# A transposed q and k: split into high and low parts in front of the transpose, or on the way out of PSUM

## The chip, the cores and the metric

The kernel runs on one core of one Trainium2 chip. The metric is the device time of one execution in microseconds (us). Engines: TensorE (PE, with its weight loads as PEld), VectorE (DVE), ScalarE (ACT), GpSimd (POOL) and SyncE (SP, which issues most DMAs).

## The reference

One decoder layer on x of 1024 tokens by 1024 features, in fp32: an RMS norm, one input projection, two attention mixers side by side, a SiLU gate on each, an output projection and the residual. What matters here:

```
proj = rms_norm(x, norm_gain) @ w_in                       # 4420 columns, split
qa, ka = rms_norm(qa, q_norm_a), rms_norm(ka, k_norm_a)    # per head of 64, 8 heads
qb, kb = rms_norm(qb, q_norm_b), rms_norm(kb, k_norm_b)    # the same for mixer B
# A: an indexer scores all causal keys; each query keeps its 256 best keys
logits = q . k * 64 ** -0.5 + bias;  p = softmax(logits)   # over the kept keys
# B: the same with three dilated windows in place of the kept keys
out = x + concat(a * silu(za), b * silu(zb)) @ w_out
```

## The kernel before

**Precision.** TensorE works on fp32r operands. An fp32 number is kept as a high part (the number rounded to fp32r) and a low part (number minus high part). A projection is three matmuls: high x high, high x low, low x high (L416 to L418). For the scores the 64 features of a head fill half of the 128 rows, so high and low part lie one above the other: k's stationary form is [high; low], q comes as [high; low] and as [low; high], and two matmuls of 128 rows give all four products (L537, L538).

**Work.** The 16 heads make 8 pairs; the order is the four pairs of mixer B, then the four of mixer A. For each pair 8 blocks of 128 tokens are projected, two blocks (a "duo") at a time. When a duo's projection is done, `finish` brings it to SBUF (`raw`), takes sums of squares, splits v and multiplies k by the norm weights of k and q together (`gk`, one row of 64 in all partitions, L448). `finish2` multiplies k by its inverse norm (L456), splits it into high and low part (L458 on ScalarE, L459 on GpSimd) and makes q (L462). `later` transposes the four 128x128 pieces of k and copies them out of PSUM (L471, L475). The queries of a duo are split by `split_q` (L502, L503) into high, low, high of 64 columns each, and `transpose_q` transposes columns 0 to 127 and 64 to 191 of each head and block (L512, L513), in two PSUM tiles, each copied out by ScalarE (L515).

Attention runs in 64 units: a pair, a duo of queries, one head. `scores` takes score chunks of up to 512 keys, adds the bias (VectorE, L544; for mixer A GpSimd first adds the selection mask, L542) and takes the exp (L554). `pt` transposes the probabilities as fp32 (L571), ScalarE copies out the high part (L575), VectorE the low part (L576); `pv` multiplies with v (L587, L589). `combine` (L609) adds up, gates and stores.

**The selectors.** For mixer A the 256 best keys of each query are found by a search over the bits of the score (L260 counts, L267 and L269 update; one block's search counts on ScalarE, L309). Its steps are a chain on VectorE that is spread over the slots of the units from before the first pair to the start of mixer A, and ends with `select_mask` (L244 to L248).

**Order.** `run_slot` writes out the order of all work by hand: each unit has a slot, and each piece a place in it (for instance `sq=0.4` for `split_q`, `qt=0.9` for `transpose_q`, `kdel` for `later`). The tile framework then orders each engine's instructions by that priority and by when their inputs are ready in its own timeline. `pace` keeps the projections from running ahead of the attention by more than a slot. PSUM: the tag "tr" has one buffer, which the transposes of k (`pk`), q (`pq`) and the gate (`pg`, L613) share. `p.eng` is GpSimd for the first six pairs and VectorE for the last two.

Of the kernel before, what the change touches and what calls it, by code (L numbers as in the profile page):

```python
# [38 lines left out]
    w=9, raw=3, praw=2, kst=3, q=4, v=5, g=5, qT=2, T=2, L=6, pt=2, s=2, proj=2, ptp=2, o=1, tr=1,  # L39
    qhl=1, kb=1, f2=3, wpos=0, kdel=(7.5, 13, 16), gw=(7, 8, 7, 8, 8, 8, 9, 9), goff=5, lead=2, late=6,  # L40
# [6 lines left out]
def kernel(ctx: ExitStack, tc: tile.TileContext, xT, x, w_idx, w_pair, w_out, gain,  # L47
                       rel_bias, onehot, lnn, qna, kna, qnb, knb, out):
# [331 lines left out]
    def head_gains():  # L380
        for nm, a, b in (("a", qna, kna), ("b", qnb, knb)):
            ga = p1.tile([P, HD], F32, name=f"gq{nm}", tag="gq", bufs=1)
            gb = cp.tile([P, HD], F32, name=f"gk{nm}")
            nc.sync.dma_start(ga, bass.AP(tensor=a.tensor, offset=a.offset, ap=[[0, P], [1, HD]]))
            nc.sync.dma_start(gb, bass.AP(tensor=b.tensor, offset=b.offset, ap=[[0, P], [1, HD]]))
            nc.vector.scalar_tensor_tensor(gb, gb, HD ** -0.5, ga, OP.mult, OP.mult)
            gk[nm] = gb
# [17 lines left out]
    def proj_item(p, tb):  # L405
# [14 lines left out]
        def finish():  # L420
# [25 lines left out]
            kk = raw[:, :, 2:4, :]  # L446
            gb = gk["a" if p.is_a else "b"]
            p.eng.tensor_tensor(kk, kk, gb.unsqueeze(1).unsqueeze(1).to_broadcast([P, 2, 2, HD]), OP.mult)  # L448
            duo["mu"] = mu

        def finish2():
# [3 lines left out]
            kk = raw[:, :, 2:4, :]  # L455
            p.eng.tensor_tensor(kk, kk, mu[:, :, 2:4].unsqueeze(3).to_broadcast([P, 2, 2, HD]), OP.mult)  # L456
            k = rg.tile([P, 2, 2, P], F32R, name="k", tag="ktok", bufs=CFG["kb"])
            nc.scalar.copy(k[:, :, :, 0:64], kk)  # L458
            p.eng.tensor_tensor(k[:, :, :, 64:128], kk, f32(k[:, :, :, 0:64]), OP.subtract)  # L459
# [5 lines left out]
        def later():  # L465
            if j == 1:
                return
            pk = ps.tile([P, 2, 2, P], F32R, name="pk", tag="tr", bufs=CFG["tr"])
            for b in range(2):
                for h in range(2):  # L470
                    nc.tensor.transpose(pk[:, h, b, :], duo["k"][:, b, h, :], identr)  # L471
            s, o = tb // 4, (tb % 4) * P
            if s not in p.k:
                p.k[s] = rg.tile([P, 2, 512], F32R, name="kst", tag="kst", bufs=CFG["kst"])
            nc.scalar.copy(p.k[s][:, :, o:o + 2 * P], f32(pk.rearrange("p h b t -> p h (b t)")))  # L475
# [22 lines left out]
    def split_q(p, s):  # L498

        q = p.q[s].rearrange("p b h d -> p (b h) d")  # L500
        hl = sb.tile([P, 4, 192], F32R, name="qhl", tag="qhl", bufs=CFG["qhl"])
        nc.scalar.copy(dup_hi(hl, 4), q.unsqueeze(2).to_broadcast([P, 4, 2, HD]))  # L502
        p.eng.tensor_tensor(hl[:, :, 64:128], q, f32(hl[:, :, 0:64]), OP.subtract)  # L503
        p.hl[2 * s] = p.hl[2 * s + 1] = hl

    def transpose_q(p, s):
        hl = p.hl[2 * s]
        for qb in (2 * s + 1, 2 * s):
            pq = ps.tile([P, 512], F32R, name="pq", tag="tr", bufs=CFG["tr"])
            for h in range(2):  # L510
                t = hl[:, 2 * (qb % 2) + h, :]
                nc.tensor.transpose(pq[:, (2 * h) * P:(2 * h + 1) * P], t[:, 0:128], identr)  # L512
                nc.tensor.transpose(pq[:, (2 * h + 1) * P:(2 * h + 2) * P], t[:, 64:192], identr)  # L513
            qt = sb.tile([P, 2, 2, P], F32R, name="qt", tag="qT", bufs=CFG["qT"])
            nc.scalar.copy(qt.rearrange("p a b c -> p (a b c)"), f32(pq))  # L515
            p.hl[qb] = qt
# [4 lines left out]
    def make_unit(p, s, h, blk):  # L521
# [4 lines left out]
        def scores(qb, ci, last):  # L526
# [8 lines left out]
            qt = p.hl[qb]  # L535
# [329 lines left out]
```

## Time and profile before

| | |
|---|---|
| median of 3 runs | 822.93 us (819.94 to 825.45) |
| profiled execution | 821.55 us, span of the core 819.7 us |
| busy, share of the span | PE 94%, PEld 80%, DVE 76%, ACT 64%, POOL 53% |
| mean granted TensorE clock | 0.988 |
| DMA | 83.33 MB, mean 102 GB/s |

The rows further down are of the profiled execution. "L571" is line 571 of the kernel before. A group of rows names engine, operation, output and inputs, count, busy time, the mean duration of one, and the engine's idle time just before such instructions with what ended it. Matmuls are pipelined, so what one costs is read from the distance of two starts and not from its duration. In the chain each stretch of time is put down to the instruction that the end was waiting for.

### The profile page before, as it was taken

The page shows a single profiled execution, that of the slowest core. Times are in us where ns is not written, and L with a number is a line of the kernel's source. Part 1 is how long each engine was busy: PE and PEld are TensorE (multiplying, and loading weights), DVE is VectorE, ACT ScalarE, POOL GpSimd, SP SyncE. Part 2 cuts the span into 40 slices and gives each one's busy share as a digit, 9 for nine tenths or more (in the row PEclk, how much of TensorE's full clock was granted, in tenths as well). Part 3 has the DMA queues.
Part 4 walks back from the last instruction along what each step waited for, and adds up shares of the span by engine and source line. Part 5 has one row for each costly group of instructions (what it writes and reads, how often), then busy time and mean ns, then how long its engine had stood idle before and what let it go on. Part 6 is the DMA issues. An engine that isn't in the chain of part 4 may idle for free.

```text
span 819.7 us, 13162 instructions
## 1 busy us (share of the span) xinstructions
PE 770.4 (94%) x4300; PEld 653.6 (80%) x4300; DVE 627.0 (76%) x1586; ACT 525.0 (64%) x1220; POOL 434.2 (53%) x452
## 2 busy tenths in 40 slices
PE   6989988999999999999997889999999998999997
PEld 5778855787888878888885778888888887888885
DVE  5935479988899999989999978657686685676631
ACT  6834464768788877778785565767676766465510
POOL 6943536417633763365237786775556566434320
PEclk9999999999999999999999899999999999999999
DMA  8679105002400320032003200240034226735776
GB/s 291 242 216 296 42 0 168 13 1 78 116 14 14 90 91 14 14 90 92 14 14 103 78 14 7 64 123 14 14 115 123 63 61 194 226 102 174 228 234 219
DMA packets 52053, 83.33 MB, mean 102 GB/s; under 512 B 5633, under 2 KB 23313, under 8 KB 51985
## 3 DMA queue, kind: packets, MB, share of 16 engines
q1 hardware_dynamic: 47376, 74.10, 29.0%
q0 software_dynamic: 4608, 8.39, 3.9%
q8 instruction: 34, 0.56, 0.3%
q14 instruction: 35, 0.28, 0.1%
HBM read 65.62 MB, written 26.29 MB: 112 GB/s over the span
## 4 chain that ended last, share of the span: by engine, by line
PE 59%; DVE 14%; ACT 3%; DMA 2%; issue 2%; POOL 1%; SPq 0%; DVEq 0%; POOLq 0%; ACTq 0%
PE pp L416 9%; PE pp L418 9%; PE pp L417 9%; PE pt L571 7%; PE po L589 6%; PE sp L537 4%; PE sp L538 4%; PE pp L644 3%; PE pp L646 3%; PE pp L645 3%; DVE jk L260 3%; DVE ptl L576 2%; DVE jk L245 1%; DVE L L544 1%; PE po L587 1%
## 5 line engine op out<-in xcount | busy, mean ns | idle before, releaser
L416 PE MATMUL pp<-wh,xh 128*128 128x512 f32 x512 | 210.0, 413 | 2.4 <-ACT praw L424 1.2
L417 PE MATMUL pp<-wl,xh 128*128 128x512 f32 x512 | 202.6, 396 | 2.6 <-POOL wl L85 2.5
L418 PE MATMUL pp<-wh,xl 128*128 128x512 f32 x512 | 202.3, 395 | 0.0
L554 ACT ACTIVATE L<-L,mn 128x512 f32<-128x512 f32 (+1 forms) x192 | 117.6, 615 | 54.0 <-DVE mn L544 52.2
L260 DVE TENSOR_SCALAR_CACHE_REDUCE jk<-sc,thr 128x512 bf16<-128x512 f32 (+4 forms) x160 | 136.3, 873 | 2.5 <-PE pt L571 2.2
L85 POOL TENSOR_TENSOR wl<-raw,wh 128x512 fp32r<-128x512 f32 x68 | 92.2, 1369 | 56.2 <-ACT wh L84 54.5
L576 DVE TENSOR_TENSOR ptl<-pt,pth 128x512 fp32r<-128x512 f32 (+1 forms) x160 | 100.2, 631 | 25.7 <-ACT pth L575 24.9
L542 POOL TENSOR_TENSOR L<-T,sc 128x512 f32<-128x512 f32 (+3 forms) x80 | 88.4, 1126 | 59.3 <-PE pt L571 42.2
L417 PEld LDWEIGHTS pp<-wl,xh 128*128 128x128 f32 x512 | 97.2, 190 | 20.2 <-POOL wl L85 4.8
L416 PEld LDWEIGHTS pp<-wh,xh 128*128 128x128 f32 x512 | 97.4, 191 | 19.4 <-ACT wh L84 2.9
L418 PEld LDWEIGHTS pp<-wh,xl 128*128 128x128 f32 x512 | 96.8, 189 | 20.1
L575 ACT CAST pth<-pt 128x512 fp32r<-128x512 f32 (+1 forms) x160 | 85.3, 541 | 37.4 <-PE pt L571 34.0
L571 PE MATMUL pt<-identr,L 128*128 128x128 f32 x576 | 89.2, 277 | 1.2 <-ACT L L554 1.0
L589 PE MATMUL po<-pth,v 128*128 128x256 f32 x256 | 73.1, 298 | 4.1 <-DVE mx L618 3.6
L589 PE MATMUL po<-ptl,v 128*128 128x256 f32 x256 | 70.6, 293 | 6.0 <-DVE ptl L576 6.0
L537 PE MATMUL sp<-kst,qt 128*128 128x512 f32 (+1 forms) x192 | 71.9, 375 | 4.3 <-DVE mn L544 4.3
L571 PEld LDWEIGHTS pt<-identr,L 128*128 128x128 f32 x576 | 66.2, 142 | 5.5 <-ACT L L554 2.4
L433 POOL TENSOR_TENSOR mu<-ss,mhalf 128x8 f32<-128x8 f32 x32 | 56.2, 1756 | 27.0 <-DVE ss L431 9.4
L84 ACT CAST wh<-raw 128x512 fp32r<-128x512 f32 x80 | 48.1, 618 | 31.3 <-DMA raw<-in_w_pair_dram 23.5
L538 PE MATMUL sp<-kst,qt 128*128 128x512 f32 (+1 forms) x192 | 67.3, 351 | 0.0
L589 PEld LDWEIGHTS po<-ptl,v 128*128 128x128 f32 x256 | 48.7, 190 | 13.9 <-DVE ptl L576 9.8
L424 ACT ACTIVATE praw<-pp,rr 128x512 f32<-128x512 f32 x64 | 43.6, 684 | 22.9 <-PE pp L418 21.2
(148 smaller groups left out, 1713.8 us busy)
## 6 DMA issues: line engine op xcount, KB each, us to landing
raw<-in_w_pair_dram SPq DMA_DIRECT2D x64, 256.0 KB, 2.8
skew<-rowd SPq DMA_DIRECT2D x16, 576.0 KB, 14.0
T<-skew SPq DMA_DIRECT2D x16, 512.0 KB, 3.8
stage<-in_x_dram SPq DMA_DIRECT2D x16, 256.0 KB, 5.4
mixh_d<-mh SPq DMA_DIRECT2D x32, 128.0 KB, 2.1
mixl_d<-ml SPq DMA_DIRECT2D x32, 128.0 KB, 1.9
raw<-in_w_out_dram SPq DMA_DIRECT2D x16, 256.0 KB, 3.4
mo<-mixh_d POOLq DMA_DIRECT2D x16, 256.0 KB, 3.5
```

Of the source, the lines that this page charges most:

```text
L85: (eng or nc.gpsimd).tensor_tensor(lo, raw, f32(hi), OP.subtract)
L260: nc.vector.tensor_scalar(jk[:, :w], sc[blocks[j]], scalar, None, op, OP.add, accum_out=cnt[:, j:j + 1])
L416: pace(nc.tensor.matmul(pp, xh[tb][:, kt, :], hi, start=(kt == 0), stop=False))
L417: nc.tensor.matmul(pp, xh[tb][:, kt, :], lo, start=False, stop=False)
L418: nc.tensor.matmul(pp, xl[tb][:, kt, :], hi, start=False, stop=(kt == KT - 1))
L537: mark(nc.tensor.matmul(sp[:, :w], qt[:, h, 0, :], kk, start=True, stop=False))
L538: nc.tensor.matmul(sp[:, :w], qt[:, h, 1, :], kk, start=False, stop=True)
L542: nc.gpsimd.tensor_tensor(l[:, :w], bias, sc[qb][:, c0:c0 + w], OP.add)
L554: nc.scalar.activation(l, l, AF.Exp, bias=mn[:, done:done + 1], scale=-1.0, accum_out=blk.den[:, j, h, c:c + 1])
L571: mark(nc.tensor.transpose(t[:, si * P:(si + 1) * P], L[qb, kb // 4][:, o:o + P], identf))
L576: nc.vector.tensor_tensor(tl[:, :w], t[:, :w], f32(th[:, :w]), OP.subtract)
L589: nc.tensor.matmul(po[:, h, :], vv, t[:, 256 * j:256 * j + 256], start=(kp == 0 and j == 0 and n == 0), stop=False)
```

## The change

k is kept as one fp32 tile of two heads side by side (no norm weights, no split), transposed whole as fp32 (two transposes in place of four), and split on the way out of PSUM: ScalarE writes the high part with the norm weights as a scale per partition, VectorE multiplies by the same scale and subtracts the high part. For the first head of a pair [high; low] results, for the second [low; high]. q is doubled in SBUF ([q, q], fp32, by `p.eng`), transposed whole (four transposes in place of eight, into one PSUM tile), and split on the way out: ScalarE copies the high part of both halves, VectorE subtracts for the low part. The two score matmuls take [high; high] and [low; low]. The norm weights come as one small array, one column for each, with features along partitions.

```diff
-    ... q=4, v=5, g=5, qT=2, T=2, L=6, ...
-    qhl=1, kb=1, f2=3, ...
+    ... q=4, v=5, g=5, qT=1, T=2, L=6, ...
+    kb=1, f2=3, ...
@@ head_gains
-        for nm, a, b in (("a", qna, kna), ("b", qnb, knb)):
-            ga = p1.tile([P, HD], F32, name=f"gq{nm}", tag="gq", bufs=1)
-            gb = cp.tile([P, HD], F32, name=f"gk{nm}")
-            nc.sync.dma_start(ga, bass.AP(tensor=a.tensor, offset=a.offset, ap=[[0, P], [1, HD]]))
-            nc.sync.dma_start(gb, bass.AP(tensor=b.tensor, offset=b.offset, ap=[[0, P], [1, HD]]))
-            nc.vector.scalar_tensor_tensor(gb, gb, HD ** -0.5, ga, OP.mult, OP.mult)
-            gk[nm] = gb
+        hg = cp.tile([P, 4], F32, name="hg")
+        nc.sync.dma_start(hg, hgain)
+        gkt = cp.tile([P, 2], F32, name="gkt")
+        nc.vector.scalar_tensor_tensor(gkt, hg[:, 0:2], HD ** -0.5, hg[:, 2:4], OP.mult, OP.mult)
+        gk["a"], gk["b"] = gkt[:, 0:1], gkt[:, 1:2]
@@ finish
-            kk = raw[:, :, 2:4, :]
-            gb = gk["a" if p.is_a else "b"]
-            p.eng.tensor_tensor(kk, kk, gb.unsqueeze(1).unsqueeze(1).to_broadcast([P, 2, 2, HD]), OP.mult)
@@ finish2
-            kk = raw[:, :, 2:4, :]
-            p.eng.tensor_tensor(kk, kk, mu[:, :, 2:4].unsqueeze(3).to_broadcast([P, 2, 2, HD]), OP.mult)
-            k = rg.tile([P, 2, 2, P], F32R, name="k", tag="ktok", bufs=CFG["kb"])
-            nc.scalar.copy(k[:, :, :, 0:64], kk)
-            p.eng.tensor_tensor(k[:, :, :, 64:128], kk, f32(k[:, :, :, 0:64]), OP.subtract)
+            k = rg.tile([P, 2, 2, HD], F32, name="k", tag="ktok", bufs=CFG["kb"])
+            p.eng.tensor_tensor(k, raw[:, :, 2:4, :], mu[:, :, 2:4].unsqueeze(3).to_broadcast([P, 2, 2, HD]), OP.mult)
@@ later
-            pk = ps.tile([P, 2, 2, P], F32R, name="pk", tag="tr", bufs=CFG["tr"])
+            pk = ps.tile([P, 2, P], F32, name="pk", tag="tr", bufs=CFG["tr"])
             for b in range(2):
-                for h in range(2):
-                    nc.tensor.transpose(pk[:, h, b, :], duo["k"][:, b, h, :], identr)
+                nc.tensor.transpose(pk[:, b, :], duo["k"][:, b].rearrange("p h d -> p (h d)"), identf)
...
-            nc.scalar.copy(p.k[s][:, :, o:o + 2 * P], f32(pk.rearrange("p h b t -> p h (b t)")))
+            pk = pk.rearrange("p b t -> p (b t)")
+            g = gk["a" if p.is_a else "b"]
+            for h, (a, b) in enumerate(((slice(0, HD), slice(HD, P)), (slice(HD, P), slice(0, HD)))):
+                ks = p.k[s][:, h, o:o + 2 * P]
+                nc.scalar.activation(ks[a], pk[a], AF.Copy, scale=g[a])
+                nc.vector.scalar_tensor_tensor(ks[b], pk[a], g[a], f32(ks[a]), OP.mult, OP.subtract)
@@ split_q becomes twice_q
-        hl = sb.tile([P, 4, 192], F32R, name="qhl", tag="qhl", bufs=CFG["qhl"])
-        nc.scalar.copy(dup_hi(hl, 4), q.unsqueeze(2).to_broadcast([P, 4, 2, HD]))
-        p.eng.tensor_tensor(hl[:, :, 64:128], q, f32(hl[:, :, 0:64]), OP.subtract)
+        p.qd = sb.tile([P, 4, 2, HD], F32, name="qd", tag="qd", bufs=1)
+        p.eng.tensor_copy(p.qd, q.unsqueeze(2).to_broadcast([P, 4, 2, HD]))
@@ transpose_q
-        for qb in (2 * s + 1, 2 * s):
-            pq = ps.tile([P, 512], F32R, name="pq", tag="tr", bufs=CFG["tr"])
+        pq = ps.tile([P, 2, 2, P], F32, name="pq", tag="tr", bufs=CFG["tr"])
+        for b in range(2):
             for h in range(2):
-                t = hl[:, 2 * (qb % 2) + h, :]
-                nc.tensor.transpose(pq[:, (2 * h) * P:(2 * h + 1) * P], t[:, 0:128], identr)
-                nc.tensor.transpose(pq[:, (2 * h + 1) * P:(2 * h + 2) * P], t[:, 64:192], identr)
-            qt = sb.tile([P, 2, 2, P], F32R, name="qt", tag="qT", bufs=CFG["qT"])
-            nc.scalar.copy(qt.rearrange("p a b c -> p (a b c)"), f32(pq))
-            p.hl[qb] = qt
+                nc.tensor.transpose(pq[:, h, b, :], p.qd[:, 2 * b + h].rearrange("p a d -> p (a d)"), identf)
+        hi = sb.tile([P, 2, 2, P], F32R, name="qh", tag="qh", bufs=CFG["qT"])
+        lo = sb.tile([P, 2, 2, P], F32R, name="ql", tag="ql", bufs=CFG["qT"])
+        nc.scalar.copy(hi, pq)
+        nc.vector.tensor_tensor(lo, pq, f32(hi), OP.subtract)
+        p.hl[s] = hi, lo
@@ scores
-            mark(nc.tensor.matmul(sp[:, :w], qt[:, h, 0, :], kk, start=True, stop=False))
-            nc.tensor.matmul(sp[:, :w], qt[:, h, 1, :], kk, start=False, stop=True)
+            mark(nc.tensor.matmul(sp[:, :w], qh[:, h, qb % 2, :], kk, start=True, stop=False))
+            nc.tensor.matmul(sp[:, :w], ql[:, h, qb % 2, :], kk, start=False, stop=True)
```

## Rows read from the trace of the kernel before

**Rows 1.** The page, part 4: the chain's share of the span by engine.
```profile
PE 59%; DVE 14%; ACT 3%; DMA 2%; issue 2%; POOL 1%; SPq 0%; DVEq 0%; POOLq 0%; ACTq 0%
```

**Rows 2.** Busy time by stage: stretch, length, busy us of each engine, clock, DMA.
```profile
120.00:480.00 360.00, 337.07 (x1897) 285.19 (x1896) 337.35 (x957) 263.53 (x603) 189.26 (x197) 0.98 0.20 57
480.00:820.00 340.00, 328.13 (x1872) 280.86 (x1870) 219.09 (x500) 194.47 (x470) 176.95 (x185) 0.99 0.39 119
...
274.00:304.00 30.00, 28.15 (x166) 23.99 (x165) 28.50 (x76) 20.92 (x49) 21.36 (x22) 1.00 0.41 123
381.00:425.00 44.00, 44.00 (x264) 38.30 (x264) 41.13 (x129) 34.48 (x82) 16.81 (x23) 1.00 0.05 13
425.00:471.00 46.00, 37.36 (x194) 30.99 (x193) 45.55 (x86) 26.52 (x60) 32.85 (x23) 0.91 0.27 81
```

**Rows 3.** The chain by line, 274 to 304 us, then 425 to 471 us.
```profile
by line: DVE jk L260 24.7%; DVE sc L324 8.3%; DVE ptl L576 7.6%; DVE thr L269 7.1%; ACT pth L575 5.8%; DVE rej L267 4.7%; DVE ss L430 4.0%; DVE L L544 4.0%; ACT wh L84 3.8%; DVE mx L618 2.9%; ACT th L441 2.8%; DVE jk L323 2.6%; issue 2.6%; 
...
by line: DVE jk L245 19.5%; issue 10.5%; DVE jk L260 9.0%; DVE sc L247 8.4%; DVE jk L244 8.1%; DVE jk L246 7.1%; DVE L L544 5.8%; DVE ptl L576 5.1%; DVE sc L248 4.0%; DVE thr L269 2.7%; DVE jk L329 2.6%; DVE ss L430 2.6%; DVE need L280 2.6%
```

**Rows 4.** Middle stage, L475 alone, then L515 alone: ScalarE busy, count.
```profile
120.00:480.00 360.00, 9.28 (x16) 0.98 0.20 57
...
120.00:480.00 360.00, 19.77 (x34) 0.98 0.20 57
```

**Rows 5.** Timeline of TensorE: start us, us, what (an fp32r burst, an fp32 burst).
```profile
303.55 0.25 PE L512 MATMUL pq<-identr,qhl 128*128 128x128 f32 x1
...
303.89 0.47 PE L537 MATMUL sp<-kst,qt 128*128 128x512 f32 x1
304.19 0.40 PE L538 MATMUL sp<-kst,qt 128*128 128x512 f32 x1
304.43 0.40 PE L537 MATMUL sp<-kst,qt 128*128 128x512 f32 x1
...
354.87 0.60 PE L571 MATMUL pt<-identr,L 128*128 128x128 f32 x4
355.23 0.48 PE L416 MATMUL pp<-wh,xh 128*128 128x512 f32 x1
355.54 0.28 PE L589 MATMUL po<-ptl,v 128*128 128x256 f32 x1
```

**Rows 6.** ScalarE groups by form; columns: busy us, mean ns, idle before, its causes.
```profile
L515 ACT CAST qt<-pq 128x512 fp32r<-128x512 f32 x64 | 37.4, 585 | 18.7 <-PE pq L513 13.8 <-PE sp L538 4.8
...
L502 ACT CAST qhl<-q 128x512 fp32r<-128x512 f32 x32 | 20.0, 626 | 0.0
...
L475 ACT CAST kst<-pk 128x512 fp32r<-128x512 f32 x32 | 18.7, 583 | 18.0 <-PE pk L471 18.0
...
L458 ACT CAST k<-praw 128x256 fp32r<-128x256 f32 x32 | 13.1, 409 | 11.0 <-POOL praw L456 9.8 <-DVE praw L456 1.1
...
L615 ACT COPY mx<-po 64x256 f32<-64x256 f32 x32 | 11.8, 369 | 8.4 <-PE po L587 7.7
```

**Rows 7.** VectorE groups by form.
```profile
L576 DVE TENSOR_TENSOR ptl<-pt,pth 128x512 fp32r<-128x512 f32 x96 | 65.4, 685 | 15.2 <-ACT pth L575 14.5
...
L617 DVE TENSOR_TENSOR mx<-mx,po 64x256 f32<-64x256 f32 x32 | 13.0, 407 | 6.9 <-ACT mx L616 4.1 <-PE sp L538 2.8
...
L186 DVE SCALAR_TENSOR_TENSOR ihl<-pi,rr,ihl 128x320 fp32r<-128x320 f32 x8 | 4.3, 542 | 5.4 <-ACT ihl L185 5.4
```

**Rows 8.** A GpSimd group by form.
```profile
L448 POOL TENSOR_TENSOR praw<-praw,gkb 128x256 f32<-128x256 f32 x16 | 11.9, 744 | 38.0 <-ACT sq L428 38.0
```

**Rows 9.** Line L443 alone; count, then ns min/median/max.
```profile
L443 DVE SCALAR_TENSOR_TENSOR g<-th,praw x32: 409/418/1507, 69.6 to 690.6; 128x256 f32<-128x256 f32 x32
```

**Rows 10.** Who TensorE waits for, whole span: us in total, times, longest.
```profile
PE po L589 <- DVE ptl L576: 6.0, 10, 1.7
...
PE pq L512 <- ACT qt L515: 4.4, 5, 2.9
...
PE pq L512 <- ACT kst L475: 3.6, 2, 2.4
```

## What I expected, written before the run

> **What bounds the kernel now.** I read the chain that ended last first, then busy time by stage, then who TensorE waits for. The chain [rows 1] is mostly TensorE (59%) but VectorE has 14%, 115 us of 819.7: a kernel with two limits. Busy time by stage [rows 2] shows where. The span falls into three: the indexer's start (0 to 120 us), the stretch in which the bitwise selectors share the chip with the dense pairs (120 to 480 us), and the rest. In the middle stage VectorE is busy 337.35 of 360 us and TensorE 337.07: both 94%, neither with room. The reader should see that they take turns inside it. From 381 to 425 us TensorE is busy 44.00 of 44 and VectorE 41.13: TensorE is the limit. From 274 to 304 VectorE has 28.50 of 30, from 425 to 471 it has 45.55 of 46 while TensorE drops to 37.36; and the chain runs through VectorE there [rows 3]: L260, L324, L576, L269 and their like from 274 to 304, L245, L260, L247, L244 from 425 to 471. From 480 us VectorE is busy only 219.09 of 340 against TensorE's 328.13: there TensorE alone decides. ScalarE (263.53) and GpSimd (189.26 of 360) bound no stage. So the question is what the change takes from TensorE, and what it gives VectorE between 120 and 480 us.
>
> There are 32 steps (8 pairs by 4 blocks of 256 tokens), each with one preparation of k (L451 to L475) and one of q (L498 to L516). The counts of L475 (one a k, 16) and L515 (two a q, 34) put 16 of k and 17 of q into the middle stage [rows 4]; the other 15 of q come later, of k some come before, since k is made ahead, and I put 12 behind and 4 before.
>
> **TensorE.** A step loses 12 transposes of fp32r operands (4 for k, 8 for q) and gains 6 of fp32 operands (2 and 4). What a burst of four costs is read from starts: the four fp32r ones and the matmul of 512 columns behind them take from 303.55 to 304.19, 0.64 us, the four fp32 ones with theirs from 354.87 to 355.54, 0.67, and such a matmul alone 0.24 (304.19 to 304.43) [rows 5]. So 0.40 and 0.43 a burst, 0.10 and 0.11 us a transpose. Per k: 0.40 - 0.22 = 0.18 us; per q: 0.80 - 0.43 = 0.37; a step 0.55, 32 steps 17.6 us. Lower bound: without what the fp32r burst costs the matmul behind it (0.34 from 303.55 to 303.89) 0.12 + 0.25 = 0.37 a step, 11.8 us. I take 15, between them, since a burst often has another short instruction behind it; by the counts 7.8 in the middle stage, 6.6 behind it, 0.6 before.
>
> The Trainium skill (FP8 and Floating Point Precision, TensorE Precision Notes) says that true fp32 takes four passes through the array; by that the six new transposes would cost as much as 24. No burst here does: 0.11 us stands against the 0.40 that four fp32r ones are [rows 5]; that result is the last rival below.
>
> **ScalarE.** A step loses L502 (0.626), L475 (0.583), L458 (0.409) and one of two L515 (0.585), together 2.20 us, and gains two 64x256 copies with a scale; L615 has that shape at 0.369 [rows 6]. Net about -1.4 us a step, 45 us in all. ScalarE bounds no stage, so I credit it only in the waits below.
>
> **VectorE.** Its gain is the price of the change. For q it now subtracts 128x512 straight from PSUM: that is L576's form, 0.685 us. For k it runs two multiply-and-subtract instructions of 64x256 from PSUM: between L617 (64x256, 0.407) and L186 (the same instruction kind with a per-partition scale, but 128x320, 0.542) [rows 7]; I take 0.43, since the length is L617's. In the middle stage that is 16 x 2 x 0.43 + 17 x 0.685 = 25.4 us (24.7 to 29.0). For the last two pairs, where VectorE does GpSimd's share as well, it also loses three instructions of 128x256 and gains one copy, in a stage where it is idle a third of the time: nothing.
>
> **GpSimd.** For the first six pairs a step loses the gain multiply (L448, 0.744) and the subtracts of k and q, of the same size and about as long, and gains a plain copy of 128x512: at least L448's 0.744 (half the size, two inputs), at most twice that [rows 8]; about 1.0, since it has one input, so -1.2 us a step. Off the chain, but some VectorE instructions stretch at times: L443, with two SBUF inputs, has a median of 418 ns and a maximum of 1507 [rows 9]. If GpSimd is the cause, some 20 us less of its 189 in the middle stage take a tenth of such tails away; I credit VectorE 2 us (0 to 4). The Trainium skill (SBUF — State Buffer, Who interferes with whom) says that an instruction of VectorE with two SBUF inputs is held up by a GpSimd one that reads SBUF, and one with at most one SBUF input is not; by that the new subtracts, which read PSUM and one SBUF tile, keep their length, and without it the sum is the same but for the 2 us.
>
> **The sum for the middle stage.** VectorE's need becomes 337.4 + 25.4 - 2 = 361 us, more than the stage has; TensorE's falls to 329. Lower end: only where the chain lies on VectorE does the addition count, everywhere else its idle time swallows it. At least 55 us of the chain are VectorE's in the stage (66% of 30 and 78% of 46, the lines listed in [rows 3]), at most the 115 of the whole span; from their middle 85/360 x 25.4 = 6.0 us, against TensorE's gain on the rest, 275/360 x 7.8 = 6.0: nothing. Middle: VectorE is bound throughout and as full as in the two stretches where it leads now (74.05 of 76, 97.4%): 361/0.974 = 370.5, +10. Upper end: it stays as full as it is over the stage (93.7%): 385, +25. I take +8, near the middle value, because the idle time that it has where TensorE leads (2.9 of 44 us) is about what the addition needs there (44/360 x 25.4 = 3.1), and hand-overs both ways will not let it run at 100%.
>
> **Waits.** Removed: TensorE waits for L515 between the two q transposes through the single "tr" buffer (4.4 us) and for L475 (3.6) [rows 10]; there is one q tile now. Added: the "tr" buffer of q and k is free only after VectorE has read it too, and the second score matmul waits for the low part from VectorE. Behind the waiting instruction the projections and the probability transposes queue on TensorE; the scheduler can put them ahead. I price 64 new hand-overs from VectorE as the existing one of L576, 6.0 us [rows 10] over its 96 largest calls [rows 7], 0.0625 us each: 4 us. Behind 480 us lies 15/32 of both: 3.8 go and 1.9 come, -2. In the middle stage they are inside the fill above. On ScalarE the high copy of q now needs all scores of the block before to be done (one buffer pair instead of two tiles); it already waits 4.8 us in all for L538 [rows 6]; behind it sit the exps of L554. The same order of size, not charged. The copies of k may have to take turns with VectorE's on one PSUM tile: nothing to 0.43 us a step, hidden as long as k is not the next thing that TensorE needs. Loading the gains: three DMAs fewer on SP's queue and one small VectorE instruction instead of two, at the start, before any pair needs them: nothing.
>
> **Total** against the profiled execution (821.55 us): +8 - 6.6 - 0.6 - 2 = 820.4. The median of the runs is 1.4 us above that execution, so 822 us: no change that can be told (about 1%, 8 us, is what a measurement of this kernel can tell).
>
> **Rivals.**
> 1. VectorE does not bind. The selectors' steps are a chain of VectorE instructions that need nothing else, so the order may pull them into its idle time (before the pairs start, and the 2.9 of 44 where TensorE leads). Then TensorE's 15 us and 3 of the net 4 us of waits come off: 822.9 - 15 - 3 = 805. For it: ScalarE, lighter by 1.4 us a step, will answer VectorE faster. Against it: it is on the chain for 115 us already. Chance 0.29.
> 2. Slower: VectorE keeps its present fill, because each of its waits repeats. Decides from the point where its need passes 360 us, which the sum says it does. +25 - 7.2 - 2 + 822.9 = 839. For it: the 22.6 us of idle time now are waits for others, not reserve. Chance 0.18.
> 3. The hand-over of q: if TensorE reaches the scores with nothing to put ahead, each step pays VectorE's subtract and the hand-over, 0.8 us, 32 x 0.8 = 26 us, less TensorE's 15: 834. Against it: TensorE has projections of the next pair in nearly every step. Chance 0.07.
> 4. The change doesn't shorten TensorE: fp32 transposes at four passes, 24 x 0.10 - 12 x 0.10 = +1.2 us a step, +38 us: 861. The fp32 burst of [rows 5] speaks against it. (The page of the Trainium skill named under TensorE would have it so.) Chance 0.02.
>
> **How the numbers follow.** The forecast has 0.44; its own range is 814 to 831. The range for 8 in 10 reaches from 803 (a little under rival 1, where TensorE's gain is at its upper bound) to 840 (rival 2). Faster by over 1% is rival 1 and a little of the forecast, 0.30; slower by over 1% is rivals 2 to 4, 0.27; within 1% 0.43.
>
> **What would show it.** VectorE busy between 120 and 480 us up by some 25 us and above 95%; the group of the q subtract at about 0.685 us and of the k one at about 0.43; ScalarE's total down by 40 us or more; TensorE's total down by some 15; the waits for L515 gone and waits for the low part of q in their place; and from 480 us to the end a stretch some 8 us shorter. Wrong would be: a middle stage that is shorter though VectorE is fuller (rival 1), a middle stage longer by 20 us with VectorE no fuller (rival 2), or 0.4 us for one fp32 transpose.

## The result, and the profile after

The changed kernel takes 885.5 us (median of 4 runs, 882.3 to 886.3) against 821.4 us of the kernel before in the same comparison: ratio 1.077, 95% interval 1.071 to 1.083. The forecast was 822, its range 803 to 840. The profiled execution has a span of 883.6 us and a mean granted TensorE clock of 0.946, where before had 819.7 and 0.988.

The page of the changed kernel (busy time by engine; TensorE's clock in tenths, 40 slices; the chain by engine):

```profile
PE 791.2 (90%) x4108; PEld 656.5 (74%) x4108; DVE 663.1 (75%) x1665; ACT 498.0 (56%) x1156; POOL 390.1 (44%) x404
...
PEclk9999988999799979997998969998999999899999
...
PE 42%; DVE 20%; DMA 4%; ACT 3%; issue 3%; POOL 0%; SPq 0%; DVEq 0%; ACTq 0%; POOLq 0%
```

TensorE runs 192 instructions fewer (six a step, as forecast) and yet is busy 20.8 us longer (770.4 before): the granted clock dips in slice after slice. TensorE's share of the chain fell from 59% [rows 1] to 42%. Busy time by stage, to be read against [rows 2], then four stretches around the start of the third pair:

```profile
120.00:480.00 360.00, 318.95 (x1654) 262.75 (x1652) 317.21 (x919) 231.94 (x523) 134.33 (x143) 0.93 0.17 50
480.00:820.00 340.00, 308.64 (x1648) 260.87 (x1649) 247.94 (x553) 184.36 (x450) 181.04 (x180) 0.94 0.28 84
...
310.00:317.00 7.00, 4.23 (x23) 3.45 (x21) 6.87 (x19) 3.17 (x8) 2.25 (x2) 1.00 0.19 70
317.00:324.00 7.00, 4.60 (x15) 3.28 (x16) 5.64 (x22) 3.83 (x10) 3.15 (x5) 0.50 0.36 112
324.00:331.00 7.00, 6.66 (x25) 5.20 (x24) 2.32 (x6) 1.81 (x3) 0.00 (x0) 0.77 0.00 0
331.00:338.00 7.00, 6.95 (x36) 5.45 (x35) 6.88 (x26) 4.93 (x12) 1.29 (x2) 1.00 0.14 40
```

VectorE, which should have become the fuller engine of the middle stage, is busy 317 of 360 us there, 20 less than before; but the changed kernel is slower and gets less of its work done by 480 us, so the two windows don't hold the same work (see "VectorE bound" below). TensorE stands still for much of 310 to 317, and for the next 7 us it is granted 0.50, the lower of its two levels (1.2 GHz). If the clock knows only 1.2 and 2.4 GHz, a mean of 0.946 is 2 x 0.054 x 883.6 = 95 us at the lower one; before it was 2 x 0.012 x 819.7 = 20 us.

Who TensorE waits for (us in total, times, longest), to be read against [rows 10]:

```profile
PE pq L507 <- DVE kst L473: 13.8, 6, 3.6
PE sp L533 <- DVE mn L540: 9.3, 15, 1.9
PE pt L567 <- ACT L L550: 8.2, 5, 3.5
PE sp L533 <- ACT qh L510: 7.2, 11, 0.9
PE po L585 <- DVE ptl L572: 6.7, 13, 1.6
...
PE pk L464 <- DVE rej L267: 3.5, 1, 3.5
```

New at the top: q's transposes (L507) wait for VectorE's last copy of k (L473), the first scores for q's high part (L510). What single instructions cost came out near the forecast (groups by form; compare [rows 6, 7]):

```profile
L472 ACT ACTIVATE kst<-pk,gkt 64x256 fp32r<-64x256 f32 x64 | 29.9, 468 | 35.9 <-PE pk L464 30.5 <-DVE kst L473 4.7
...
L473 DVE SCALAR_TENSOR_TENSOR kst<-pk,gkt,kst 64x256 fp32r<-64x256 f32 x64 | 30.9, 483 | 11.3 <-ACT kst L472 9.4
...
L511 DVE TENSOR_TENSOR ql<-pq,qh 128x512 fp32r<-128x512 f32 x32 | 21.9, 686 | 6.0 <-ACT qh L510 5.7
```

**Where a pair begins.** The timeline shows the loss best. The kernel before, from the gate's product of one pair (`pg`) to q of the next:

```profile
295.71 0.41 PE L613 MATMUL pg<-identr,g 128*128 128x128 f32 x2
295.96 0.49 PE L571 MATMUL pt<-identr,L 128*128 128x128 f32 x3
296.20 0.48 PE L416 MATMUL pp<-wh,xh 128*128 128x512 f32 x1
...
299.48 0.40 PE L418 MATMUL pp<-wh,xl 128*128 128x512 f32 x1
299.71 0.28 PE L589 MATMUL po<-pth,v 128*128 128x256 f32 x1
299.83 0.46 PE L471 MATMUL pk<-identr,k 128*128 128x128 f32 x4
...
302.19 0.28 PE L512 MATMUL pq<-identr,qhl 128*128 128x128 f32 x1 [1.26 <-ACT kst L475]
```

The changed kernel at the same place:

```profile
313.56 0.38 PE L609 MATMUL pg<-identr,g 128*128 128x128 f32 x2
...
313.96 0.27 PE L583 MATMUL po<-ptl,v 128*128 128x128 f32 x1
...
317.14 0.41 DVE L615 TENSOR_TENSOR mx<-mx,pg 128x256 f32<-128x256 f32 x1
...
317.69 0.66 PE L464 MATMUL pk<-identr,k 128*128 128x128 f32 x2 [3.46 <-DVE rej L267]
...
318.38 0.47 ACT L472 ACTIVATE kst<-pk,gkt 64x256 fp32r<-64x256 f32 x1 [0.40 <-PE pk L464]
...
319.44 0.48 DVE L473 SCALAR_TENSOR_TENSOR kst<-pk,gkt,kst 64x256 fp32r<-64x256 f32 x1
...
319.96 0.47 ACT L472 ACTIVATE kst<-pk,gkt 64x256 fp32r<-64x256 f32 x1 [0.45 <-DVE kst L473]
...
320.87 0.49 DVE L473 SCALAR_TENSOR_TENSOR kst<-pk,gkt,kst 64x256 fp32r<-64x256 f32 x1
...
321.51 1.09 PE L507 MATMUL pq<-identr,qd 128*128 128x128 f32 x4
...
323.27 1.22 PE L533 MATMUL sp<-kst,qh 128*128 128x512 f32 x2 [0.67 <-ACT qh L510]
```

All three tiles pass through the "tr" bank. In both kernels VectorE reads `pg` (L615, L619 before) only after some selection steps that stand ahead of it in its queue. Before, 15 projections (296.20 to 299.71) stand between `pg` and `pk` on TensorE and cover that. In the changed kernel none do: `pk` is the next instruction, TensorE waits 3.46 us for the bank, then k's copies go ScalarE, VectorE, ScalarE, VectorE one behind the other until 321.36, then `pq`, then q's copy. When work is there again, the clock is at 0.50. TensorE's queue had been given another order with the new instructions.

This start shows both waits, but it is not the usual one. Of the 35.8 us that TensorE idles in the seven such stretches of the changed kernel (table below), 5.4 stand before `pk`, at two starts; 13.8 stand before `pq`, where VectorE's last copy of k is waited for, at six; 4.7 stand before the first score, some 0.7 at each.

### The profile page after: what moved, and what is told of

Same layout as the page of the kernel before. It is cut to its first block, busy times and chain, and to the rows that moved or that the text cites. A ratio compares the mean times of both kernels' runs of the same rounds, so it can differ in the third digit from the quotient of the medians.

```text
span 883.6 us, 12724 instructions
## 1 busy us (share of the span) xinstructions
PE 791.2 (90%) x4108; PEld 656.5 (74%) x4108; DVE 663.1 (75%) x1665; ACT 498.0 (56%) x1156; POOL 390.1 (44%) x404
## 4 chain that ended last, share of the span: by engine, by line
PE 42%; DVE 20%; DMA 4%; ACT 3%; issue 3%; POOL 0%; SPq 0%; DVEq 0%; ACTq 0%; POOLq 0%
PE pp L415 6%; PE pp L416 6%; PE pp L417 6%; PE pt L567 5%; DVE jk L260 4%; PE po L585 4%; PE sp L533 3%; PE sp L534 2%; PE pp L640 2%; DVE ptl L572 2%; PE pp L641 2%; PE pp L642 2%; DVE L L540 2%; DMA out_dram<-xr 2%; PE pq L507 1%
## 5 line engine op out<-in xcount | busy, mean ns | idle before, releaser
L415 PE MATMUL pp<-wh,xh 128*128 128x512 f32 x512 | 217.2, 425 | 7.5 <-ACT praw L423 5.8
L416 PE MATMUL pp<-wl,xh 128*128 128x512 f32 x512 | 208.0, 406 | 1.0 <-POOL wl L85 1.0
L417 PE MATMUL pp<-wh,xl 128*128 128x512 f32 x512 | 206.0, 403 | 0.0
L415 PEld LDWEIGHTS pp<-wh,xh 128*128 128x128 f32 x512 | 101.1, 198 | 25.9 <-ACT praw L423 6.2
L417 PEld LDWEIGHTS pp<-wh,xl 128*128 128x128 f32 x512 | 99.9, 195 | 21.7
L416 PEld LDWEIGHTS pp<-wl,xh 128*128 128x128 f32 x512 | 100.9, 197 | 19.8 <-POOL wl L85 2.8
L567 PE MATMUL pt<-identr,L 128*128 128x128 f32 x576 | 91.5, 281 | 8.9 <-ACT L L550 8.2
L533 PE MATMUL sp<-kst,qh 128*128 128x512 f32 (+1 forms) x192 | 68.0, 380 | 16.4 <-DVE mn L540 9.3
L534 PE MATMUL sp<-kst,ql 128*128 128x512 f32 (+1 forms) x192 | 64.3, 351 | 0.1
L619 POOL TENSOR_TENSOR ml<-mx,mh 128x256 fp32r<-128x256 f32 x32 | 24.3, 760 | 90.7 <-ACT mh L618 58.8
```

The source lines that it names most:

```text
L415: pace(nc.tensor.matmul(pp, xh[tb][:, kt, :], hi, start=(kt == 0), stop=False))
L416: nc.tensor.matmul(pp, xh[tb][:, kt, :], lo, start=False, stop=False)
L417: nc.tensor.matmul(pp, xl[tb][:, kt, :], hi, start=False, stop=(kt == KT - 1))
L533: mark(nc.tensor.matmul(sp[:, :w], qh[:, h, qb % 2, :], kk, start=True, stop=False))
L567: mark(nc.tensor.transpose(t[:, si * P:(si + 1) * P], L[qb, kb // 4][:, o:o + P], identf))
```

## The experiments

Of each run: its time; how many projections TensorE has between the gate's product and the next pair's first score, at the seven starts of a pair; TensorE's idle time in these seven stretches together (counted from the starts and ends in each trace); and the mean clock. Each batch was compared with runs of the kernel before, 819.4 to 825.4 us.

| kernel | us | projections in the stretch | idle, us | clock |
|---|---|---|---|---|
| before | 821.4 | 15 15 15 15 15 15 27 | 5.8 | 0.988 |
| after | 885.5 | 0 0 0 0 5 6 15 | 35.8 | 0.946 |
| k_only | 855.5 | 0 0 0 0 6 4 27 | 27.3 | 0.958 |
| q_only | 835.7 | 15 15 15 15 15 15 12 | 9.5 | 0.976 |
| k_seq | 866.9 | 0 0 0 0 13 15 27 | 25.1 | 0.960 |
| kq_free | 850.1 | 23 24 27 21 32 35 27 | 12.6 | 0.976 |
| q_ahead | 884.3 | 0 0 0 0 5 6 15 | 36.6 | 0.954 |
| warm | 893.7 | 0 0 0 0 12 12 27 | 27.6 | 0.961 |
| k_ptp | 833.9 | 34 28 40 21 36 33 29 | 5.0 | 0.979 |
| b_ptp | 813.8 | 33 33 33 23 33 33 23 | 2.6 | 0.987 |
| konly_ptp | 833.2 | 33 33 33 33 33 33 20 | 2.7 | 0.979 |

**One half of the change alone.** k_only takes `split_q`, `transpose_q` and the score operands from before, q_only the k path from before.

k_only: 

> The change for k alone, q prepared as before. Theory A (load): the loss of 64 us comes from VectorE's added work, so it splits as that work does, 31 us for k and 22 for q: about +37 us here, and VectorE's busy share in the selector stage near 95%. Theory B (hand-over): the last k of a pair and then its first q pass the single PSUM buffer 'tr' at the start of each pair; it is held until VectorE has read it, TensorE has nothing else left to do and its clock falls. k is in that chain with four instructions one behind the other, so k alone gives most of it, +40 us or more, with the loss at the pair starts.

q_only: 

> The change for q alone, k prepared as before. Theory A: about +26 us. Theory B: the chain at a pair's start loses one of its two q tiles and gets VectorE's 0.69 us only before the second score matmul: between -10 and +20 us.

k alone costs 3.8% (2.9 to 4.7), some 30 us and less than either expectation; q alone costs 1.4% (0.4 to 2.5), as theory B has it. Together they cost 7.7%, more than the sum. Who TensorE waits for in k_only:

```profile
PE pq L510 <- ACT qt L513: 8.9, 12, 1.2
PE pq L510 <- DVE kst L473: 7.4, 5, 2.2
...
PE pk L464 <- DVE mx L617: 6.2, 3, 3.2
```

With k's half the order of before is gone (no projections in the first four stretches); with q's half it stays, and q's transposes wait for k's copy no longer than before.

**VectorE's load.** dve_load and load_tied are the kernel before with useless reductions on VectorE; in load_tied they read the fresh k and q, so that they fall where the change puts its subtracts:

```diff
             nc.scalar.copy(p.k[s][:, :, o:o + 2 * P], f32(pk.rearrange("p h b t -> p h (b t)")))
+            for h in range(2):
+                busy(f32(p.k[s][:, h, o:o + 2 * P]))
...
             p.hl[qb] = qt
+        busy(f32(qt.rearrange("p a b c -> p (a b c)")))
```

dve_load: 

> The kernel before with three more VectorE instructions a step that nobody waits for (two reductions over 320 elements behind the copy of k, one over 512 behind that of q, results unused), about 1.65 us a step like the added work of the change. Theory A: most of the 64 us, +40 to +60. Theory B: under +15 us, since nothing on TensorE's way waits for VectorE more often than before.

load_tied: 

> The first load test showed VectorE's busy time unchanged at 338 us between 120 and 480 us and 35 us more before 120: its free reductions were all done early, so it did not load the stage in question. Here the reductions read what they follow (two of 256 the fresh columns of k, one of 512 the fresh q), so they can't come early; results unused, 1.5 us a step. Theory A (load): VectorE's busy time in the middle stage up by some 15 us or its stage longer, +25 us or more in all. Theory B (hand-over): under +15 us.

dve_load took 835.1 us, ratio 1.014 (1.003 to 1.025), but tells nothing of the middle stage: its reductions ran before 120 us (VectorE there 105.6 us against 70.6), and from 120 to 480 it was no fuller (338.0). load_tied did what was meant, and took 824.3 us, ratio 1.004 (0.9995 to 1.008). Its middle stage:

```profile
120.00:480.00 360.00, 334.53 (x1881) 282.61 (x1879) 350.24 (x993) 260.73 (x595) 178.69 (x193) 0.97 0.20 56
```

VectorE at 97% of the stage costs 3 us, by the interval no more than 7. These reductions are 13 us in this window, about half of what the change adds, and nobody waits for their results; VectorE's sum alone is not what the change pays.

**The order of k's copies.** k_seq:

```diff
+            for h, (a, b) in enumerate(hs):
+                nc.scalar.activation(p.k[s][a, h, o:o + 2 * P], pk[a], AF.Copy, scale=g[a])
             for h, (a, b) in enumerate(hs):
                 ks = p.k[s][:, h, o:o + 2 * P]
-                nc.scalar.activation(ks[a], pk[a], AF.Copy, scale=g[a])
                 nc.vector.scalar_tensor_tensor(ks[b], pk[a], g[a], f32(ks[a]), OP.mult, OP.subtract)
```

> The changed kernel with k's copies in another order: both ScalarE copies first, then both VectorE subtracts, in place of copy, subtract, copy, subtract, where the second copy was seen waiting for the first subtract. Theory A: no change against the changed kernel (885). Theory B: the chain at each pair's start is shorter by a hand-over each way, 10 to 25 us come back.

866.9 us: about 19 of the 64 us come back with the order of two lines, with the same work. The waits of `pq` at the seven starts fall from 13.8 to 4.5 us. Not all of it need be the copies' turns: 6 of the 19 us are gained up to the fifth pair's first score, the others behind it, where TensorE's queue also has another order (13, 15 and 27 projections in place of 5, 6 and 15).

**Without the selection.** Both kernels with `sel=()`.

nosel_b: 

> The kernel before without the selectors: the search for each query's 256 best keys is left out (raw index scores are added in place of the mask). Both theories: faster than before by what VectorE's 107 us on the way cost, about 770 to 790 us. It is the partner of the next run.

nosel_a: 

> The changed kernel without the selectors (the same part is left out). VectorE then has room everywhere. Theory A: the change no longer costs, it gains TensorE's 10 to 15 us against the partner run. Theory B in its strict form (the chain through the single buffer costs by its own length): still slower than the partner by 20 us or more. If the chain costs only because VectorE's queue is long when it is asked, the two are within 10 us.

789.9 and 822.2 us: the change still costs 32 us where VectorE is little more than half busy. Waits in nosel_a:

```profile
PE pq L507 <- DVE kst L473: 15.9, 7, 3.1
PE sp L533 <- ACT qh L510: 6.0, 10, 0.7
```

The chain of copies costs by its own length. With the selection the change costs twice as much, and 52 of its 64 us fall in the first four pairs, where VectorE selects; without it every pair loses some, 2 to 7 us each.

**ScalarE alone reads PSUM.** In kq_free ScalarE copies k out once in full precision, and its high part and the subtract are made from that copy; of q it copies out the high part and the full number, each from PSUM. The subtracts run on GpSimd in the first six pairs.

> The changed kernel with VectorE taken out of both copies: ScalarE writes k (scaled) and q as fp32 to SBUF beside the high parts, and the subtracts read SBUF and run on GpSimd (VectorE in the last two pairs). Adds ScalarE 0.5 us and 0.6 us a step and GpSimd about 2.4 us. Theory A and theory B both have most of the 62 us come back, below 840; if the buffer is what holds TensorE, the waits for pq behind kst go below 5 us, and TensorE's shorter transposes may put it below the kernel before (815).

850.1 us, ratio 1.032 (1.017 to 1.046): 35 us back, not below 840 as both theories had it. The long waits for `pq` are gone from the list, and 21 to 35 projections stand in the stretches.

**The bank, q's lead, and the clock.** k_ptp is one line:

```diff
-            pk = ps.tile([P, 2, P], F32, name="pk", tag="tr", bufs=CFG["tr"])
+            pk = ps.tile([P, 2, P], F32, name="pk", tag="ptp", bufs=CFG["ptp"])
```

> The changed kernel with one line changed: the transposes of k take a bank of the pair of PSUM banks that the transposed exponentials use, and leave the single bank to g and q. If the loss comes from the hand-overs through the single bank (g's product must be read before k may be transposed, k's four copies must end before q may be transposed), the idle time of 3 to 4 us before k's transposes where a pair begins goes, and those before q's that wait for the last copy of k shrink; eight pairs at 1 to 3 us and the half clock behind them make 10 to 25 us, so 860 to 875. If the copies' own length is what counts (the first score needs them whichever bank they come from), the wait only moves to the first score: 880 to 890.

833.9 us: about 51 of the 64 us, far more than expected. Its TensorE where the third pair begins:

```profile
299.16 0.41 PE L609 MATMUL pg<-identr,g 128*128 128x128 f32 x2
299.32 0.48 PE L417 MATMUL pp<-wh,xl 128*128 128x512 f32 x1
...
306.63 0.38 PE L464 MATMUL pk<-identr,k 128*128 128x128 f32 x2
306.76 0.37 PE L585 MATMUL po<-pth,v 128*128 128x256 f32 x1
306.97 0.60 PE L507 MATMUL pq<-identr,qd 128*128 128x128 f32 x4
308.72 0.50 PE L533 MATMUL sp<-kst,qh 128*128 128x512 f32 x1 [1.15 <-ACT qh L510]
```

28 projections stand between `pg` and the first score, and the only wait left is 1.15 us for q's copy.

q_ahead (`qt=0.7`, two buffers for q's high part): 

> The changed kernel with q transposed 0.2 of a step earlier and two buffers for q's high part, so that its ScalarE copy and VectorE subtract should be over when TensorE comes to the first score. If TensorE's wait for q's two copies makes the loss inside the pairs (23 us by the first scores of the pairs), most of it comes back: 860 to 870, and the waits of the first score for q's high part, 7.2 us, fall under 2. If that loss is made elsewhere (the row minimum, the low part of the exponentials), the time stays at 880 to 890.

884.3 us: nothing. But the edit did not move them: in its trace all 32 groups of q's transposes have as many scores ahead of them in TensorE's queue as in the changed kernel, and 31 as many instructions up to the next score; where a pair begins they stand directly ahead of the first score. So whether an earlier place of q's transposes would help was not tested.

warm (six useless products around each `pq`): 

> The changed kernel with useless work for TensorE around q's transposes: three products of 512 columns with an identity ahead of them and three behind, in a bank of the scores, 192 in all; at 0.23 us each (the spacing of such products in a stretch at full clock) they take 44 us. If the fall of the granted clock behind the idle stretches is a large part of the loss, the clock rises from 0.946 and the time stays the same or falls in spite of the added work: 860 to 890. If idle time alone is the loss, the part that falls outside it, some 20 to 40 us, is added: 905 to 925, and the clock stays at 0.95.

893.7 us, between the two expectations: 44 us of added work cost 8 us. TensorE is busy 823.3 us, 32 more than in the changed kernel and not 44, at a clock of 0.961, and the waits have partly filled. That speaks for the fall of the clock as a part of the loss: with it milder, the rest of TensorE's work takes some 12 us less, an estimate from 44 and 32. It is no clean measure, since the last three starts also have more projections here (12, 12 and 27).

combo (k_seq, k_ptp and q_ahead together): 

> The changed kernel with three edits together: both ScalarE copies of k ahead of both subtracts (19 us alone), k's transposes in the other pair of banks, q's transposes 0.2 of a step earlier with two buffers for the high part. If hand-overs and the half clock that follows them are the whole loss, the three add up to 45 to 70 us: 815 to 840, near the kernel before; below it only if the work that TensorE is spared, 15 us by the prediction's sum, also shows. If something else in the change costs the time, it stays over 850.

831.2 us: the three don't add up; the edit of the bank gives nearly all.

**What is left with the bank freed.** b_ptp is the same line in the kernel before; konly_ptp is k_only with it; combo_e is combo without q's part; free_ptp is kq_free with it.

b_ptp: 

> The kernel before with one line changed as in the last kernels: the transposes of k take a bank of the pair that the transposed exponentials use, not the single one. If the single bank binds only where k's copies are long (the changed kernel), the kernel before gains little: 812 to 824. If it binds in both, the gain of 51 us seen in the changed kernel is not an undoing of the change's damage but a gain of its own, and this kernel falls under 805.

konly_ptp: 

> Only the part of the change that concerns k (q is split and transposed as before), with k's transposes in the pair of banks. k alone in the single bank took 855.5. If the single bank was all that k's part cost, it comes to the kernel before or under it, 808 to 824, since TensorE is spared 64 of its transposes of k and GpSimd its two products of k; and the 12 us that the changed kernel with this edit still has over the kernel before belong to q. If k's two turns of ScalarE and VectorE cost by themselves, it stays at 828 to 840.

combo_e: 

> The changed kernel with k's transposes in the pair of banks and both ScalarE copies of k ahead of both subtracts, q left as the change has it. With q ahead as well it took 831.2, with the bank alone 833.9. If the order of k's copies matters only through the single bank (19 us there), it gives nothing more here: 830 to 836. If the copies' own length still delays the first scores, it falls to 822 to 828.

free_ptp: 

> The changed kernel with k's transposes in the pair of banks, and k and q copied out of PSUM once by ScalarE in full precision, the high parts and the subtracts made from that copy in SBUF (by GpSimd in the first six pairs): VectorE loses 25 us of the middle stage, the two hand-overs out of PSUM become one, but q's low part comes later. If what remains (12 us) is VectorE's fuller queue, it falls under 824; if it is the time until q's two parts are there, it rises to 838 to 850.

b_ptp took 813.8 us, ratio 0.989 (0.986 to 0.992): 8 us off the kernel before, the fastest version that keeps the selection. The line gives 8 us there and 51 in the changed kernel, so 43 of the 51 are damage of the change undone. konly_ptp took 833.2, combo_e 833.6, free_ptp 839.5. With the bank freed q's half costs nothing on top of k's (833.9 against 833.2), but k's half still costs 19 us over b_ptp.

combo_g and b_ptp_g take the gate's product off VectorE (in the first six pairs):

```diff
+            if p.i < CFG["late"]:
+                nc.gpsimd.tensor_tensor(th, th, raw[:, :, 6:8, :], OP.mult)
+                nc.gpsimd.tensor_tensor(g, th, raw[:, :, 6:8, :], OP.add)
+            else:
```

combo_g: 

> The changed kernel with the three edits (831.2) and the gate's last product, 17 times 0.64 us on VectorE in the stretch from 120 to 480 us, made by GpSimd in two products: VectorE loses 11 us there, GpSimd, busy 150 of 360 us, gains some 25. If what remains of the loss is VectorE's work while it selects (from the first scores to those of the fifth pair the three-edit kernel is 19 us longer than the kernel before with the bank freed, with VectorE busy 19 us more and idle 18 and 17 us), 7 to 11 us come back: 820 to 825. If it is the time from product to product at k and q, nothing: 828 to 835.

b_ptp_g: 

> The control: the kernel before with k's transposes in the pair of banks (813.8) and the same product moved to GpSimd, which is busier there, 190 of 360 us. If VectorE's sum bounds the middle stage in every version, it gains as much, 803 to 807; if it is only near the bound here, it gains half of it or less, 808 to 815; above that if GpSimd comes late with k and q.

834.5 us (combo 831.2) and 818.7 us (b_ptp 813.8): no gain in either, and the control lost 5 us. This does not clear VectorE's sum, which hardly fell: from the first score to the fifth pair's first score VectorE is busy 334.5 us in combo_g against 336.9 in combo, and 318.4 in b_ptp_g against 319.5 in b_ptp. The product took 8.7 to 10.1 us less, but other instructions of VectorE took longer.

## Why the prediction was wrong

**The step that failed** is "Waits". It priced a hand-over from VectorE at 0.0625 us, and k's copies taking turns at "nothing to 0.43 us a step, hidden as long as k is not the next thing that TensorE needs". At each pair's start k is just that: there `pq` waited 13.8 us in all for k's last copy, and `pk` 5.4 us for its bank. From the gate's product to the first score of the next pair TensorE idled 5.8 us in all seven starts before, 35.8 after; its idle time over the whole span rose from 49 to 92 us. By the first scores, 44 of the 64 us are lost between a pair's last unit and the next pair's first, 23 inside pairs (the first unit of each pair alone makes 18), and 5 are gained ahead of the first pair. With the bank freed in both kernels (k_ptp against b_ptp) the 44 are gone (-2), and 23 inside pairs remain.

**The supposition under it** was rival 3's "Against it: TensorE has projections of the next pair in nearly every step". The trace of before showed that, but as a property of one order of TensorE's queue, not of the work: the changed instructions came with another order. k_seq's own trace fits: at the fifth and sixth start, where it has 13 and 15 projections, TensorE idles 1.7 and 1.3 us; the changed kernel with 5 and 6 idles 4.0 and 4.0. But the count does not decide alone. At the changed kernel's seventh start 15 projections stand ahead of `pk`, and TensorE still idles 5.3 us, 2.59 of them before `pq`; nosel_a has 15 at its first start and waits 2.82 us before `pq`. Projections ahead of `pk` cover the wait for the bank and not the one for k's copies. That the order alone, with nothing else touched, gives this loss was not tried: k_ptp frees the bank and gets another order at the same time. What is shown is that with k's transposes in another bank the changed kernel is 51 us faster and the kernel before 8, and that 19 of the 35.8 us of idle time where a pair begins stand right at the hand-overs through the one bank.

The Trainium skill (PSUM — Partial Sum Buffer, Engine vs sequencer instructions) says that matmuls start in program order. The trace agrees: from 314.23, the end of the product that started at 313.96, nothing starts on TensorE until `pk` has its bank at 317.69. The Trainium skill (the same page, PSUM bank collisions raise a hardware error) says that two engines must not be in one bank in the same partitions at once, and that in different groups of 32 partitions they may. That does not account for the turns of k's copies: the second ScalarE copy reads partitions 64 to 127 of `pk` and the first VectorE subtract partitions 0 to 63, and yet the copy starts at 319.96, when the subtract (319.44, 0.48 us long) is over, after a wait of 0.45 us for it. So this turn is an order that the program was given, and no run here has the two overlap.

**The clock** was no term of the sum at all. 95 us at the lower level against 20 can cost up to half of the difference, 37 us, if all of it were work. TensorE's busy time agrees in kind: 20.8 us up, with less work.

**VectorE bound (+8), rival 2, and the middle stage above 95%.** The added work was priced about right. From the first score to the fifth pair's first score both kernels do the same work (the changed kernel's row follows that of before):

```profile
125.50:468.60 343.10, 325.70 (x1851) 276.66 (x1851) 322.52 (x924) 255.18 (x585) 177.14 (x186) 0.99 0.20 57
...
120.90:516.10 395.20, 341.17 (x1757) 280.81 (x1757) 352.00 (x991) 246.09 (x557) 155.03 (x161) 0.93 0.18 51
```

VectorE is busy 29.5 us longer there (25.4 forecast), but the stretch grew by 52.1 us, and VectorE's share of it fell from 94% to 89%. So its fill does not bound the changed kernel; load_tied filled the stage of the kernel before to 350 us at no cost that can be told. Rival 2's sign, "a middle stage longer by 20 us with VectorE no fuller", came true, and most of it went away with the bank, which rival 2 does not name.

**TensorE (-15)**: the price of a transpose was right; the saving does not show in the time. Four fp32 transposes of q take 0.35 us from start to next start in k_ptp; the fp32r burst of [rows 5] takes 0.34 in the same measure (303.55 to 303.89):

```profile
291.92 0.60 PE L507 MATMUL pq<-identr,qd 128*128 128x128 f32 x4
292.27 0.36 PE L585 MATMUL po<-ptl,v 128*128 128x256 f32 x1
```

So rival 4 is excluded, and with it the four passes of the Trainium skill (FP8 and Floating Point Precision, TensorE Precision Notes) for transposes: here the measurement decides. How much of the 15 us was saved no run isolates: k_ptp is as busy as b_ptp (767.3 and 767.9 us) at a lower clock.

**Sizes.** q's subtract: 0.685 forecast, 0.686 measured. k's: 0.43 and 0.483, for [rows 7] have no multiply-and-subtract of 64 rows. ScalarE's copy with a scale: 0.369 and 0.468. ScalarE lost 27 us in all (525.0 to 498.0), not 45. The wait for q's low part, expected in place of L515's, hardly came; that for its high part did (7.2 us).

**Still open**: the 19 us that k's half costs with the bank freed. They lie in the stage in which VectorE selects. The rows of b_ptp and k_ptp, from the first score to the fifth pair's:

```profile
124.70:461.40 336.70, 324.23 (x1849) 276.21 (x1848) 319.53 (x920) 255.06 (x585) 175.30 (x185) 0.98 0.20 57
...
120.80:484.40 363.60, 330.18 (x1750) 273.89 (x1750) 339.86 (x971) 241.90 (x549) 148.73 (x154) 0.96 0.18 54
```

konly_ptp takes 355.4 us there, with VectorE busy 332.8. Behind this stage nothing is lost: 350.6 us in b_ptp, 345.5 in k_ptp, 353.3 in konly_ptp. VectorE is busy 93 to 95% of the stage in all three, as rival 2 would have it. But its load alone doesn't make the loss: load_tied, with 339.2 us of VectorE in the stage, takes 349.0, 6 more than before, and free_ptp, with 326.0, takes 356.8. The copies' order and ScalarE as the only reader of PSUM gave nothing; an earlier q and less work on VectorE were not really tested by their runs, and both kernels without the selection and with the bank freed were not run. One of its waits, in konly_ptp:

```profile
199.46 0.40 PE L417 MATMUL pp<-wh,xl 128*128 128x512 f32 x1
204.76 0.55 PE L587 MATMUL po<-pth,v 128*128 128x256 f32 x1 [4.91 <-DVE mx L616]
```

VectorE has the awaited addition behind a subtract of k and three counts of the selection, from 199.90 to 203.77, though ScalarE's copy for it is done at 199.62. Whether such places make up the 19 us was not tested.

## What to carry to other kernels

Before a copy out of PSUM is split between two engines, ask what else needs that bank, and what stands ahead of the copies in the queue of each engine; cover seen in the old trace belongs to the old order of the queue, so it is no constant of a forecast. A chain of small hand-overs at a place where TensorE had nothing else cost its length here, and then a stretch at the lower clock. Compare busy shares over the same work and not over the same microseconds, and read from the trace that an edit of the order moved what it was to move. The cheapest test is to give the tile another bank: one line, 51 us here, and 8 us in the kernel that seemed not to need it.

## What was not expected of the hardware

A stop of TensorE of 3.5 us was followed by a stretch of 7 us with a granted clock of 0.50 and one of 0.77. 44 us of useless products cost 8 us, at a mean clock of 0.961 in place of 0.946. And four transposes of fp32 operands took 0.35 us, where four of fp32r took 0.34.
